# Two decoder layers on one core: where the route weights are made and how alpha x enters the sums

## The chip, the cores and the metric

The kernel runs on one core of a Trainium2 chip, and the metric is the time of one execution on the device in microseconds. PE is TensorE, DVE is VectorE, ACT is ScalarE, POOL is GpSimd and SP is SyncE, which here only issues DMAs. A median of three runs is given, and one profiled execution, from which all rows come.

## What is computed

Two post-norm layers over 256 tokens of width 1024 in fp32. Layer 0 mixes with a gated MLP and latent attention, layer 1 with sparse attention; each mixer is followed by a norm, then a mixture of 32 experts (4 groups of 8; one group, two experts of it for a token) and another norm.

```python
def reference(x, ...):
    for layer in range(DEPTH):
        mix = ab_mixer(x, ...) if layer % 2 == 0 else nsa_mixer(x, ...)
        x = layer_norm(DN_ALPHA * x + mix, ln1_g[layer], ln1_b[layer])
        ffn = hier_moe(x, moe_w_rg[layer], ..., moe_w_down[layer])
        x = layer_norm(DN_ALPHA * x + ffn, ln2_g[layer], ln2_b[layer])
    return x
```

`hier_moe` takes the group by argmax, the two best experts of the group, and weights their outputs with the softmax over the two times the group's probability. Both sums that a norm takes contain alpha x.

## The kernel before

All weights come from HBM through one ring of 23 places of 1 MB in SBUF (class `Ring`). `free` gives places back and `pump` at once issues the next loads in a fixed order on SP, so a load starts when a place is free and SP has come to it. Each layer's experts take 96 such loads: 8 quads of 4 experts, each 8 pieces for the gate and up products and 4 for the down product.

The tokens stand in two halves of 128 (t = 0, 1), and x in two halves of 512 columns (`HALF`). `project` multiplies the mixer's output with its output weights into four PSUM tiles `acc[t][h]`. For each half `products(t, 0)` opens them with `mm(acc[t][h], aident, x[:, t, HALF[h]], True, False)`, where `aident` is the identity times alpha, so alpha x enters by PE; then products with the weights, split into a high and a low part, follow (`mm3`). Most steps of `project` are placed among the mixer's own work by the automatic scheduler; from `close_mixer` on the order is the one written out by hand, and each engine executes its instructions in that order.

`close_mixer` takes the sums out of PSUM (`raw`: ACT copies to x, DVE's statistics read PSUM), normalises without gain and bias, computes the router's logits by PE, and `route` finds the experts on DVE (the maxima, and the one-hot sums in `selb`). `route` returns a function `weights`, which makes the route weights `w32` later. `rank` numbers the tokens of each expert, `places` makes one-hot matrices of a quad's token places (L1358), and `pick` selects the quad's tokens from x with them on PE, in two halves of the depth, each evacuated from PSUM (L1383, L1385 with gain and bias, otherwise L1377). Two functions are left for later: the second half of the first selection together with the four steps `affine`, which put gain and bias on x, and `rest`, which calls both `weights` (L1254 to L1264) and then `back`. It also opens the expert sums `acc2` with matmuls by the zero matrix `zerob`.

`moe_layer` runs the quads. `quad(i)` calls `gate_up`, 8 steps k of gate and up products; before each step `between(k)` runs small work: in quad 0 the functions left over (from k = 4 on), the additions of the quad before into the expert sums (`scatter`, at k = 2 and 4), and the one-hots of the next quad (`places`, at k = 4). After them comes, in quad 0, `rest`; then `activate` on ACT and DVE, the next quad's selection (`pick`, 32 products), the turning of the hidden values (`turn_hidden`, L1449), in quad 0 the products of `aident` with x into the expert sums, `back` for the next quad, and `down`. `back` multiplies the one-hots with the route weights on DVE (L1393), transposes the one-hots on PE (L1397), adds up the weights for each place by four one-column products, and copies the results (L1401, L1403). Most matmuls are issued in the helper `mm`, line 182. Between the sixth and the seventh quad a branch (L1299) looks whether an expert got more tokens than its places hold.

Of the kernel before, what the change touches and what calls it, by code (L numbers as in the profile page):

```python
# [142 lines left out]
def trunk(ctx, tc, a, out):  # L143
# [109 lines left out]
    aident = consts.tile([128, 128], F32, name="aident")  # L253
    idb = consts.tile([128, 128], BF16, name="idb")
    zerob = consts.tile([128, 128], BF16, name="zerob")
# [11 lines left out]
    def more_constants():  # L267
# [4 lines left out]
        V.memset(zerob, 0.0)  # L272
        V.tensor_scalar(aident, ident, ALPHA, None, op0=ALU.mult)
# [174 lines left out]
    def project(l):  # L448
# [7 lines left out]
        def products(t, i):  # L456
            k = ks[i]
            if i == 0:
                for h in range(2):
                    mm(acc[t][h], aident, x[:, t, HALF[h]], True, False)  # L460
            y = [part[:, t * 128:(t + 1) * 128] for part in ys[k]]
            for h in range(2):
                w = held[i][h] if i in SMALL else [part[:, HALF[h]] for part in held[i]]
                mm3(acc[t][h], y, w, False, i == KC - 1)
# [11 lines left out]
    def close_mixer(l, rb, acc, step, products):  # L476
# [4 lines left out]
        def raw(t):  # L481

            for h in range(2):
                S.activation(x[:, t, HALF[h]], acc[t][h], AF.Copy)
            return x[:, t], *stats(acc[t])
# [41 lines left out]
        for h in range(2):  # L527
            mm(acc2[0][h], zerob, idb[:, None, :].to_broadcast([128, 4, 128]), True, False)
        warm(2)
# [5 lines left out]
        for h in range(2):  # L535
            mm(acc2[1][h], zerob, idb[:, None, :].to_broadcast([128, 4, 128]), True, False)
        warm(W1[0])
# [11 lines left out]
        def rest():  # L549
            weights0()  # L550
            weights1()
            return (xg, *back(0, rt, dd, "O"))

        return rt, acc2, (xg, [second] + affines, rest)
# [835 lines left out]
    def back(q, rt, dd, tr, often=True):  # L1390

        d, dw = dd[:, 0:256], (p2() if dd.shape[1] == 256 else dd[:, 256:512])[:, 0:256]
        V.tensor_tensor(dw.rearrange("p (t e s) -> p t e s", t=2, e=4), d.rearrange("p (t e s) -> p t e s", t=2, e=4),  # L1393
                        rt[1][:, :, 4 * q:4 * q + 4, None].to_broadcast([128, 2, 4, 32]), op=ALU.mult)
        p = ps(tr)
# [13 lines left out]
    def gather(q, rt, base, tr):  # L1409
# [5 lines left out]
        return xg, *back(q, rt, dd, tr, often)  # L1415
# [62 lines left out]
    def moe_layer(l, rt, acc, begun):  # L1478
# [3 lines left out]
        gs, late = [(begun[0], None, None)], begun[1:]  # L1482
# [7 lines left out]
        def quad(i):  # L1490
# [4 lines left out]

            def between(k):
                nonlocal rb
                if i == 0 and k >= KC // 2:
                    late[0].pop(0)()
                    if k == KC - 1:  # L1500
                        late[0].pop(0)()
                if k in (2, 4):
                    flush(2)
                if k == 4:
                    dds.append(places(nq, rt, 0.0))
                if k == 5 and i == 3 and l == 0:
# [3 lines left out]
            if i == 0:  # L1510
                gs = [late[1]()]
            hs = activate(hp, [g[2] for g in gs])
            ngs, hts = [], None
            for c in range(nn):
                xg = halves_of(w4())
                pick(dds[c], xg)()
# [176 lines left out]
```

## Time and profile before

| what | us |
|---|---|
| median of 3 runs (700.06 to 701.95) | 700.41 |
| the profiled execution | 700.38 |
| its span, first to last instruction | 698.7 |
| PE busy in it | 619.1 |
| DVE busy | 284.3 |
| ACT busy | 204.5 |

The span holds the first mixer up to about 111 us, its routing up to 120, the experts of layer 0 up to about 323, the second mixer up to 468, its routing up to 477, and the experts of layer 1 up to about 687, with the last norm behind them. PE's busy time counts matmuls whose ends are modelled and overlap. The mean granted clock is 0.956 of 2.4 GHz.

### The profile page before, as it was taken

The page shows a single profiled execution, that of the slowest core. Times are in us where ns is not written, and L with a number is a line of the kernel's source. Part 1 is how long each engine was busy: PE and PEld are TensorE (multiplying, and loading weights), DVE is VectorE, ACT ScalarE, POOL GpSimd, SP SyncE. Part 2 cuts the span into 40 slices and gives each one's busy share as a digit, 9 for nine tenths or more (in the row PEclk, how much of TensorE's full clock was granted, in tenths as well). Part 3 has the DMA queues.
Part 4 walks back from the last instruction along what each step waited for, and adds up shares of the span by engine and source line. Part 5 has one row for each costly group of instructions (what it writes and reads, how often), then busy time and mean ns, then how long its engine had stood idle before and what let it go on. Part 6 is the DMA issues. An engine that isn't in the chain of part 4 may idle for free. (4 is left out here: it accounts for less than half of the span.)

```text
span 698.7 us, 11137 instructions
## 1 busy us (share of the span) xinstructions
PE 619.1 (89%) x4459; PEld 386.7 (55%) x4459; DVE 284.3 (41%) x709; ACT 204.5 (29%) x514; POOL 49.6 (7%) x56
## 2 busy tenths in 40 slices
PE   7799999799999685887999999999799899897883
PEld 5678676464555141423988776685554554644331
DVE  4757736522222120206848897444422212312116
ACT  5554534121111010103546676431111111202011
POOL 4611000000000000002420000000000000000002
PEclk9999999989999988997999999999899999999797
DMA  8946879949999999999498450399689999999961
GB/s 344 418 184 247 334 264 380 398 189 425 419 420 418 423 420 416 421 420 416 161 422 342 127 235 1 129 394 401 280 353 420 420 422 421 420 419 422 414 266 60
DMA packets 34068, 235.62 MB, mean 337 GB/s; under 512 B 3920, under 2 KB 4688, under 8 KB 6224
## 3 DMA queue, kind: packets, MB, share of 16 engines
q1 hardware_dynamic: 34000, 234.75, 82.7%
q8 instruction: 38, 0.62, 0.4%
q14 instruction: 30, 0.25, 0.1%
HBM read 233.69 MB, written 1.05 MB: 336 GB/s over the span
## 5 line engine op out<-in xcount | busy, mean ns | idle before, releaser
L182 PE MATMUL psC<-ring,w 128*32 128x512 f32 (+1 forms) x1040 | 132.5, 618 | 24.5 <-PEq L1299 13.1
L182 PEld LDWEIGHTS psC<-ring,w 128*32 128x32 f32 (+1 forms) x1040 | 31.2, 114 | 90.0 <-issue 48.5
L182 PE MATMUL psA<-ring,ring 128*128 128x256 f32 (+1 forms) x480 | 80.1, 315 | 0.0
L182 PE MATMUL psT<-ring,p 128*32 128x512 f32 (+1 forms) x608 | 68.8, 587 | 3.1 <-DMA ring<-in_moe 2.2
L182 PEld LDWEIGHTS psA<-ring,ring 128*128 128x128 f32 x480 | 67.5, 193 | 6.5 <-issue 1.8
L182 PEld LDWEIGHTS psT<-p,x 128*128 128x128 f32 x512 | 64.5, 208 | 10.9 <-issue 10.1
L182 PE MATMUL psT<-p,x 128*128 128x128 f32 x512 | 67.3, 295 | 0.0
L1437 DVE SCALAR_TENSOR_TENSOR p<-p,psC 128x256 f32<-128x256 f32 x16 | 6.7, 421 | 133.5 <-ACT p L1436 133.3
L317 DVE TENSOR_TENSOR p<-psT,p 128x256 fp32r<-128x256 f32 x72 | 30.5, 424 | 62.8 <-ACT p L316 62.8
L1436 ACT ACTIVATE p<-psC 128x256 f32<-128x256 f32 x16 | 6.1, 383 | 170.2 <-PE psC L182 170.2
L316 ACT ACTIVATE p<-psT 128x256 fp32r<-128x256 f32 x72 | 27.5, 383 | 63.2 <-PE psT L182 42.2
L290 POOL TENSOR_TENSOR sm<-sm,mhalf 128x1 f32<-128x1 f32 (+1 forms) x12 | 7.7, 647 | 511.4 <-DVE sm L287 280.6
L182 PEld LDWEIGHTS psA<-p,k 128*128 128x128 f32 x144 | 25.2, 192 | 30.1 <-issue 17.6
L182 PE MATMUL psA<-p,k 128*128 128x256 f32 x144 | 39.4, 313 | 1.6 <-DVE sm L1560 1.6
L312 DVE TENSOR_TENSOR ring<-ring,ring 128x1024 fp32r<-128x1024 f32 (+1 forms) x28 | 36.0, 1301 | 8.0 <-ACT ring L311 7.7
L182 PEld LDWEIGHTS psT<-ring,p 128*32 128x32 f32 x608 | 17.3, 111 | 37.6 <-issue 25.3
L182 PE MATMUL psS<-ring,ring 128*128 128x416 f32 (+3 forms) x128 | 32.0, 384 | 2.0 <-ACT ring L311 1.5
L182 PE MATMUL psO<-ring,ring 128*64 128x256 f32 (+3 forms) x248 | 32.2, 349 | 1.1 <-DVE ring L333 0.7
L311 ACT ACTIVATE ring<-ring 128x1024 fp32r<-128x1024 f32 (+1 forms) x32 | 31.8, 1031 | 3.6 <-issue 1.3
L182 PE MATMUL psS<-p,k 128*128 128x256 f32 x144 | 29.9, 288 | 0.0
L1377 DVE COPY w<-psT 128x512 f32<-128x512 f32 x16 | 11.1, 691 | 44.2 <-PE psT L182 44.2
L1111 ACT ACTIVATE ring<-psS,sm 128x128 f32<-128x128 f32 (+1 forms) x64 | 26.2, 420 | 7.8 <-DVE sm L1102 7.7
(282 smaller groups left out, 844.4 us busy)
## 6 DMA issues: line engine op xcount, KB each, us to landing
ring<-in_moe SPq DMA_DIRECT2D x192, 1024.0 KB, 19.5
ring<-in_m SPq DMA_DIRECT2D x23, 1024.0 KB, 10.0
ring<-in_vec SPq DMA_DIRECT2D x2, 1024.0 KB, 18.1
ring<-in_m SPq DMA_DIRECT2D x2, 832.0 KB, 6.0
x<-in_x SPq DMA_DIRECT2D x2, 512.0 KB, 5.2
out<-x SPq DMA_DIRECT2D x4, 256.0 KB, 2.0
ring<-in_m SPq DMA_DIRECT2D x1, 768.0 KB, 15.0
ring<-in_m SPq DMA_DIRECT2D x1, 736.0 KB, 18.9
```

The source lines that it names most:

```text
L182: T.matmul(o, lhsT, rhs, start=start, stop=stop, skip_group_check=True)
L290: G.tensor_tensor(r, t, mhalf[:, :n], op=ALU.pow)
L311: S.activation(hi, src, AF.Copy)
L312: (sub or V).tensor_tensor(lo, src, hi.bitcast(F32), op=ALU.subtract)
L316: S.activation(hi, src, AF.Copy)
L317: V.tensor_tensor(lo, src, hi.bitcast(F32), op=ALU.subtract)
L1111: S.activation(p[:, i * w:(i + 1) * w], sx[c, u][:, i * w:(i + 1) * w], AF.Exp, bias=nb[:, i0 + i:i0 + i + 1], accum_out=su[:, i0 + i:i0 + ...
L1377: (S.activation(dst, p[0], AF.Copy) if f == 0 else V.tensor_copy(dst, p[0]))
L1436: S.activation(e, p[:, 0:256], AF.Tanh, scale=0.5)
L1437: V.scalar_tensor_tensor(e, e, 1.0, p[:, 0:256], op0=ALU.add, op1=ALU.mult)
```

## The change

The products with `aident` and with `zerob` go, and with them both constants. In `raw` DVE adds alpha x to the mixer's sum and writes x, and the statistics read x. The expert sums are begun by ACT, which writes alpha x into the PSUM tiles (`residual`: the first half of the columns at k = 7 of the first quad, the second after the next quad's `back`). The route weights and their product with the first quad's one-hots (`shares`) are made at k = 1 of the first quad's products. In all quads the one-hots are multiplied with the weights where they are made (`onehots`, `weighted`), and `back` finds them ready. In place of the `zerob` products as many warming matmuls stand. `router_prep` of the second layer moves from the fourth quad to the sixth. The scratch for dynamic DMAs is 1024 in place of 512.

```diff
         def products(t, i):
             k = ks[i]
-            if i == 0:
-                for h in range(2):
-                    mm(acc[t][h], aident, x[:, t, HALF[h]], True, False)
...
-                mm3(acc[t][h], y, w, False, i == KC - 1)
+                mm3(acc[t][h], y, w, i == 0, i == KC - 1)
...
         def raw(t):
             for h in range(2):
-                S.activation(x[:, t, HALF[h]], acc[t][h], AF.Copy)
-            return x[:, t], *stats(acc[t])
+                V.scalar_tensor_tensor(x[:, t, HALF[h]], x[:, t, HALF[h]], ALPHA, acc[t][h], op0=ALU.mult, op1=ALU.add)
+            return x[:, t], *stats([x[:, t, HALF[h]] for h in range(2)])
...
-        for h in range(2):
-            mm(acc2[0][h], zerob, idb[:, None, :].to_broadcast([128, 4, 128]), True, False)
-        warm(2)
+        warm(4)
...
-        for h in range(2):
-            mm(acc2[1][h], zerob, idb[:, None, :].to_broadcast([128, 4, 128]), True, False)
-        warm(W1[0])
+        warm(W1[0] + 2)
...
-        def rest():
+        def shares():
             weights0()
             weights1()
-            return (xg, *back(0, rt, dd, "O"))
-
-        return rt, acc2, (xg, [second] + affines, rest)
+            return weighted(0, rt, dd, p2()[:, 0:256])
+
+        return rt, acc2, (xg, [second] + affines, shares, lambda dw: (xg, *back(dd, dw, "O")))
...
-    def back(q, rt, dd, tr, often=True):
-
-        d, dw = dd[:, 0:256], (p2() if dd.shape[1] == 256 else dd[:, 256:512])[:, 0:256]
+    def weighted(q, rt, d, dw):
+
         V.tensor_tensor(dw.rearrange("p (t e s) -> p t e s", t=2, e=4), d.rearrange("p (t e s) -> p t e s", t=2, e=4),
                         rt[1][:, :, 4 * q:4 * q + 4, None].to_broadcast([128, 2, 4, 32]), op=ALU.mult)
+        return dw
+
+    def back(d, dw, tr, often=True):
+
         p = ps(tr)
...
+            def residual(h):
+                for t in range(2):
+                    S.activation(acc[t][h], x[:, t, HALF[h]], AF.Copy, scale=ALPHA)
+
+            def onehots(c):
+                dd = places(nq, rt, -32.0 * c)
+                dds.append((dd[:, 0:256], weighted(nq, rt, dd[:, 0:256], dd[:, 256:512])))
+
             def between(k):
                 nonlocal rb
+                if i == 0 and k == 1:
+                    late[1] = late[1]()
                 if i == 0 and k >= KC // 2:
                     late[0].pop(0)()
                     if k == KC - 1:
                         late[0].pop(0)()
+                        residual(0)
                 if k in (2, 4):
                     flush(2)
                 if k == 4:
-                    dds.append(places(nq, rt, 0.0))
-                if k == 5 and i == 3 and l == 0:
+                    onehots(0)
+                if k == 5 and i == 5 and l == 0:
                     rb = router_prep(1, "T")
 
             hp = gate_up(l, q, [g[0] for g in gs], between)
             if i == 0:
-                gs = [late[1]()]
+                gs = [late[2](late[1])]
             hs = activate(hp, [g[2] for g in gs])
             ngs, hts = [], None
             for c in range(nn):
                 xg = halves_of(w4())
-                pick(dds[c], xg)()
+                pick(dds[c][0], xg)()
                 if c + 1 < nn:
-                    dds.append(places(nq, rt, -32.0 * (c + 1)))
+                    onehots(c + 1)
                 if c == 0:
                     hts = turn_hidden(hs)
-                    if i == 0:
-                        for t in range(2):
-                            for h in range(2):
-                                mm(acc[t][h], aident, x[:, t, HALF[h]], False, False)
-                ngs.append((xg, *back(nq, rt, dds[c], "O")))
+                ngs.append((xg, *back(*dds[c], "O")))
+            if i == 0:
+                residual(1)
```

## Rows read from the trace of the kernel before

**Rows 1.** Page, part 2: GB/s of the DMAs in 40 equal slices of the span

```profile
GB/s 344 418 184 247 334 264 380 398 189 425 419 420 418 423 420 416 421 420 416 161 422 342 127 235 1 129 394 401 280 353 420 420 422 421 420 419 422 414 266 60
```

**Rows 2.** Stretches: length, busy us (instructions) by engine, granted clock, DMA share, GB/s

```profile
140.00:150.00 10.00, 10.00 (x43) 8.23 (x43) 2.08 (x5) 1.64 (x4) 0.00 (x0) 0.69 0.41 168
150.00:160.00 10.00, 10.00 (x86) 4.39 (x85) 2.28 (x6) 1.92 (x5) 0.00 (x0) 1.00 0.70 270
...
500.00:510.00 10.00, 10.00 (x66) 5.82 (x69) 1.61 (x4) 2.13 (x5) 0.00 (x0) 0.94 0.16 50
```

**Rows 3.** The same columns for single microseconds of layer 0's hole

```profile
143.00:144.00 1.00, 1.00 (x7) 1.00 (x6) 0.00 (x0) 0.20 (x1) 0.00 (x0) 0.50 0.71 295
...
146.00:147.00 1.00, 1.00 (x9) 0.95 (x8) 0.26 (x1) 0.04 (x1) 0.00 (x0) 0.94 0.02 8
...
152.00:153.00 1.00, 1.00 (x12) 0.26 (x8) 0.00 (x0) 0.16 (x1) 0.00 (x0) 1.00 0.28 49
```

**Rows 4.** Timeline, layer 0: start, length, engine, line, operation, count [idle before, releaser]

```profile
134.51 0.44 PE L1397 MATMUL psO<-ident,k 128*128 128x128 f32 x2
...
139.95 6.76 PE L182 MATMUL psT<-p,x 128*128 128x128 f32 x32
...
150.85 3.64 PE L182 MATMUL psT<-ring,p 128*32 128x512 f32 x32
...
151.97 3.76 SPq L124 DMA_DIRECT2D ring<-in_moe  x5
```

**Rows 5.** Timeline of the same stretch in layer 1

```profile
483.07 0.73 DVE L1383 TENSOR_SCALAR w<-psT,col 128x128 f32<-128x128 f32 x2 [4.82 <-PE psT L182]
...
491.10 0.44 PE L1397 MATMUL psO<-ident,k 128*128 128x128 f32 x2
...
495.76 1.02 PE L182 MATMUL psO<-oneh,p 128*128 128x1 f32 x4 [4.23 <-DVE p L1393]
...
496.64 5.94 PE L182 MATMUL psT<-p,x 128*128 128x128 f32 x32
...
506.73 3.64 PE L182 MATMUL psT<-ring,p 128*32 128x512 f32 x32
```

**Rows 6.** Timeline of layer 1's seventh quad, selection to down product

```profile
658.83 3.84 PE L182 MATMUL psT<-p,x 128*128 128x128 f32 x32
...
663.78 0.61 PE L182 MATMUL psO<-oneh,p 128*128 128x1 f32 x4 [0.68 <-DVE p L1393]
664.32 3.64 PE L182 MATMUL psT<-ring,p 128*32 128x512 f32 x32
```

**Rows 7.** Waits (us, times, longest): whole span, then 235 to 262, then 649 to 690

```profile
PE psO L182 <- DVE p L1393: 18.6, 16, 4.2
...
PE psC L182 <- DMA ring<-in_moe: 5.4, 6, 1.4
...
PEld psC L182 <- DMA ring<-in_moe: 0.6, 2, 0.3
```

**Rows 8.** Stretches, products with aident alone: PE, PEld, DVE busy, clock, DMA share, GB/s

```profile
78.00:92.00 14.00, 4.19 (x8) 1.35 (x8) 0.00 (x0) 1.00 0.68 254
418.00:445.00 27.00, 2.14 (x4) 0.61 (x4) 0.00 (x0) 1.00 0.00 1
```

**Rows 9.** Timeline: an addition from PSUM in mixer 0, and layer 1's second token half

```profile
74.01 0.69 DVE L706 SCALAR_TENSOR_TENSOR p<-psC,ring 128x512 f32<-128x512 f32 x1 [0.20 <-PE psC L182]
...
467.44 1.30 ACT L484 ACTIVATE x<-psS 128x512 f32<-128x512 f32 x2 [1.51 <-PE psS L182]
...
468.07 1.39 DVE L413 BATCH_NORM_STATS2 sm<-psS 128x6 f32<-128x512 f32 x2 [1.14 <-ACT x L484]
...
472.16 0.26 DVE L510 SCALAR_TENSOR_TENSOR sm<-psC,sm,sm 128x40 f32<-128x40 f32 x1
```

**Rows 10.** End of layer 1: a microsecond of the stream, and the last down product

```profile
676.00:677.00 1.00, 1.00 (x16) 0.18 (x8) 0.00 (x0) 0.00 (x0) 0.00 (x0) 1.00 0.16 66
...
684.15 1.07 PE L182 MATMUL psT<-ring,p 128*32 128x256 f32 x16
```

More of the change, by code (lines that the diff above doesn't have):

```diff
@@ L252, in trunk @@
     ident = consts.tile([128, 128], F32, name="ident")
-    aident = consts.tile([128, 128], F32, name="aident")
     idb = consts.tile([128, 128], BF16, name="idb")
-    zerob = consts.tile([128, 128], BF16, name="zerob")
     maskb = consts.tile([128, 128], BF16, name="maskb")
@@ L271, in more_constants @@
         V.memset(oneb, 1.0)
-        V.memset(zerob, 0.0)
-        V.tensor_scalar(aident, ident, ALPHA, None, op0=ALU.mult)
         V.tensor_copy(maskb, tri[:, 128:256])
@@ L1414, in gather @@
         pick(dd, xg)()
-        return xg, *back(q, rt, dd, tr, often)
+        return xg, *back(dd[:, 0:256], weighted(q, rt, dd[:, 0:256], dd[:, 256:512]), tr, often)
     def gate_up(l, q, xgs, between):
@@ L1481, in moe_layer @@
         order = QUADS[l]
-        gs, late = [(begun[0], None, None)], begun[1:]
+        gs, late = [(begun[0], None, None)], list(begun[1:])
         pending = []
@@ L1684 @@
     arrays = {f"in_{k}": np.ascontiguousarray(v) for k, v in pack(inputs).items()}
-    nc = _bacc.Bacc("TRN2", target_bir_lowering=False, num_devices=1, dynamic_dma_scratch_size=512)
+    nc = _bacc.Bacc("TRN2", target_bir_lowering=False, num_devices=1, dynamic_dma_scratch_size=1024)
     args = {k[3:]: nc.dram_tensor(k, v.shape, mybir.dt.from_np(v.dtype), kind="ExternalInput").ap()
```

## The prediction

> **What bounds the kernel now.** I read the DMA row of the page first, then busy time by stretch, then the timeline where the DMA falls silent, then the waits. In the expert layers the weight stream runs at about 420 GB/s [rows 1], but it has one hole in each of them: 168 and 270 GB/s in 140 to 160 us, 50 GB/s in 500 to 510 us [rows 2]. The ring is full there: the eight gate/up products of the first quad free eight places, and then nothing is freed until the first down product. In layer 0 the next loads are issued at 151.97, 1.1 us after that product begins at 150.85 [rows 4]; the stream thins out at 143.7, moves next to nothing in 146:147 and begins again in 152:153 [rows 3].
>
> What keeps the down product back is PE's own chain [rows 4, 5]. The quad's last gate/up product is followed at 491.10 by the transposes of `back`; then PE waits 4.23 us, up to 495.76, for the route weights, a chain of small DVE and ACT steps, comes back at half clock, so that 32 selecting products take 5.94 us (6.76 in layer 0) where they take 3.84 at full clock [rows 6], runs the residual products, and reaches the down product at 506.73: 15.63 us. In layer 0 it is 134.51 to 150.85, 16.34 us.
>
> After the hole the two layers differ. In layer 0 PE catches up with the stream and waits for it (5.4 us in 235 to 262) [rows 7]: its end is the stream's end. In layer 1 PE hardly waits for a load up to the end, 0.6 us of weight loads in 649 to 690 [rows 7], and the stream is ahead: its last bytes pass in 676:677, and 1 MB of them, 2.5 us at 420 GB/s, is the layer norm's gains and biases, so the last expert weights are there by about 674.5, while their product begins at 684.15 [rows 10]. 9.6 us are in hand there. So layer 0 gains what the stream gains, layer 1 what PE gains.
>
> **The change part by part.** *Weights and residual in layer 0.* With the weights ready and the residual on ACT, the way from the last gate/up product to the down product is: `back` (two transposes 0.44, four one-column products 0.54, overlapping: 0.8), then what the same chain takes in quad 6 at full clock from the first selecting product at 658.83 to the down product at 664.32, 5.49, less its 0.68 wait [rows 5, 6]: 5.6 us. PE saves 16.34 - 5.6 = 10.7 us. The loads then come out at about 141.3 instead of 151.97, ahead of 143.7, so the hole closes. It is worth (420 - 168) x 10/420 + (420 - 270) x 10/420 = 9.6 us of stream by bytes [rows 2]. The 16 DMA engines do not stop together, and a load is there only with its slowest: by the silence from about 146.5 to 152.5 [rows 3] it is 6 to 7. I take 8.7, nearer to the bytes, since all engines have to carry them; ends 6.5 and 9.6.
>
> *The same in layer 1.* There PE counts: 15.63 - 5.6 = 10.0 us; ends 9.0 and 10.4. The stream moves by (420 - 50) x 10/420 = 8.8 us as well, so PE may gain up to 9.6 + 8.8 = 18.4 before it has to wait.
>
> *Where the weights go.* The chain lasts about as long as PE's wait for it, 4.2 us. It is put on DVE behind the first selection's evacuation and ahead of the second's at 483.07, before which DVE has nothing for 4.82 us [rows 5]; ACT has nothing there either. Cost nothing, cover 0.6 us; behind it stand the second evacuation, the next quad's one-hots and the norm's gains, and PE's products from k = 4 wait for the first of these. If the chain ran longer, every us beyond 0.6 would cost one.
>
> *One-hots times weights earlier in all quads.* PE waited for this multiplication (L1393) 16 times, 18.6 us [rows 7]; the two long waits are counted above, 14 short ones of about 0.7 are left. The multiplication moves to k = 4 beside gate/up products, or ahead of its use by 32 selecting products. In layer 0 PE's time is hidden by the stream: 0. In layer 1 eight waits fall away, 5.6 us; ends 4 and 6.
>
> *Residual on ACT.* Four writes of 128x512 into PSUM a layer. No row shows ACT writing PSUM; the nearest is its copy from PSUM, 1.30 for two [rows 9]. The first two lie under the gate/up products, the others before the first down evacuation, which can't come before four products of the down step are done. A gain excludes itself, since ACT does nothing there now; at double the price the evacuation would be about 1 us late, and the sums that wait for it stand behind two more gate/up products. 0 taken; end 1 us per layer.
>
> *Mixers: alpha x.* Removed from PE: eight 512-column products, 3.4 us by their spacing of 0.43, a layer. In layer 0 they lie in 78 to 92 us [rows 8], where attention's tail still makes PE wait for ACT and DVE; two pairs stand in such waits, two hold up work that is ready, 1.7 us. In layer 1 half of them stand in 418 to 445 us [rows 8], between products that wait for DVE; the rest is earlier, in the same mixer: 0. Ends 0.9 and 3.4, 0 and 1.7. The Trainium skill ("Trainium Kernel Development and Optimization", Performance Expectations) says that matmul busy time is a bad measure because matmuls are pipelined. By busy time alone both layers would give the whole 3.4, and the sum below would be 29.7; the gaps between dependent rows agree with the page.
>
> Added to DVE: two 128x512 sums in place of ACT's copies, 0.69 each by L706, which also reads PSUM. For the second token half ACT's copies started at 467.44 and the statistics at 468.07; now the sums take 1.38 and the statistics follow at 468.8, 0.7 later, and first routing and the logits' scaling at 472.16 stand behind them on DVE [rows 9]. For the first half DVE waits for PE's logits anyway. +0.7 us a layer; ends 0 and 0.8.
>
> *The rest.* Clearing by matmul becomes as many warming matmuls; two constants fall away; `router_prep` of layer 1 moves from quad 3 to quad 5, where PE waits for the stream, and its load stays in place on SP's queue; the larger DMA scratch serves DMAs that GpSimd issues, and the page lists none. All 0.
>
> **Sum.** Layer 0: 8.7 + 1.7 - 0.7 = 9.7. Layer 1: 10.0 + 5.6 + 0 - 0.7 = 14.9. Together 24.6 us. The profiled execution took 700.38 us (span 698.7 and 1.7 around it), the median is 700.41: 675.8 us.
>
> **The rivals.**
> 1. *Layer 1's stream does not move with PE.* If its hole closes on paper only, PE has 9.6 us in hand and then waits: layer 1 gives 9.6 - 0.7 = 8.9, together 18.6, 681.8 us. For it: the stream is saturated from 510 us on. Against it: the hole is silence, with places full.
> 2. *The mixers give all that PE carried*: 3.4 + 1.7 more than 1.7 in sum, 672.4 us.
> 3. *The weights do not move.* DVE works in order; if something ahead of the chain holds it until the second evacuation, only the residual products (3.4 a layer) and the short waits go: 3.4 + 1.0 + 3.4 + 5.6 - 0.7 = 12.7, 687.7 us.
> 4. *Slower: holes in the mixers' tails.* The products taken out were work that PE could do while it waited. A hole of 4.2 us was followed by the lower clock level (granted 0.69 on the mean of 140 to 150 us, so some six of the ten at 1.2 GHz) [rows 2], which cost 2.1 to 2.9 us on 32 products [rows 4 to 6]; hole and clock make about 6.7. Four of them eat up the 24.6, and 703 us result. In 78 to 92 and 418 to 445 us the granted clock is 1.00, 2.4 GHz [rows 8], and what goes there is 3.4 us in a layer, in four pieces: four long holes are unlikely. The Trainium skill ("TensorE: Matmul & The Clock Gate", HAM oscillation) warns of this: idle gaps return the array to half rate. The trace agrees behind the route weights; no row here shows it in the mixers.
>
> **How the numbers follow.** Forecast 0.72; rival 1 0.10; rival 2 0.08; rival 3 0.06; rival 4 0.02; something between 3 and 4 that ends within 0.3% (what a measurement can tell from no change, 2.1 us) 0.02. The ends of the terms: all good 9.6 + 3.4 + 10.4 + 6 + 1.7 = 31, all bad 6.5 + 0.9 + 9 + 4 - 1.6 - 2 = 17. They will not all fall together; 671 to 682 holds most of the forecast and rivals 1 and 2. Faster 0.96, same 0.02, slower 0.02.
>
> **What would show it.** Right: no DMA silence behind the first quad, from about 110 us up to the end of layer 0's experts at 420 GB/s; granted clock 1.00 there; some 5.6 us from the last gate/up product to the down product; no wait for the weighted one-hots; layer 1 without waits for loads. Wrong: a wait of the second selection's evacuation for the weights; PE waiting for loads late in layer 1; the time from the last mixer product to the first gate/up product longer by more than 0.8; holes in the mixers' tails.

## The result: 671.8 us instead of 700.4

The changed kernel takes 671.79 us (median; single runs 668.4 to 673.8) against 700.41 before. The ratio is 0.958, 95% interval 0.954 to 0.9625. A second series of five runs gave 671.57 and a ratio of 0.959 (0.958 to 0.9605). The forecast was 675.8 with a range of 671.0 to 682.0: the sign, the size and the range hold, but the kernel gained 28.6 us where the sum said 24.6. The profiled execution took 672.46 us (span 670.7), so 27.9 us are to be found between the two profiles.

The page's DMA row of the changed kernel (GB/s in 40 slices) and four stretches (length, busy us and instructions by engine, granted clock, DMA share, GB/s), two in each layer behind the first quad's gate/up products, answer [rows 1] and [rows 2]:

```profile
GB/s 346 417 202 249 353 279 362 393 423 419 419 421 421 422 420 415 421 419 421 103 423 414 174 247 7 1 380 380 415 421 419 421 421 421 421 421 418 418 413 95
```

```profile
130.00:140.00 10.00, 10.00 (x91) 7.23 (x93) 4.58 (x10) 3.70 (x9) 0.00 (x0) 1.00 1.02 425
140.00:150.00 10.00, 10.00 (x92) 4.02 (x84) 2.35 (x6) 1.15 (x3) 0.00 (x0) 1.00 1.01 422
490.00:500.00 10.00, 10.00 (x88) 4.82 (x81) 2.18 (x6) 0.77 (x2) 0.00 (x0) 1.00 1.01 422
500.00:510.00 10.00, 10.00 (x91) 5.78 (x93) 3.46 (x9) 2.91 (x7) 0.00 (x0) 1.00 1.02 423
```

Both holes (slices of 189 and 280 in the row of before) are gone: the stream runs at 422 to 425 GB/s, PE is busy throughout, its granted clock is 1.00. The timelines of the same places answer [rows 4] (layer 0, with the next loads on SP's queue) and [rows 5] (layer 1); columns start, length, engine, line, operation, count:

```profile
132.23 0.44 PE L1389 MATMUL psO<-ident,k 128*128 128x128 f32 x2
132.87 3.82 PE L182 MATMUL psT<-p,x 128*128 128x128 f32 x32
137.40 3.64 PE L182 MATMUL psT<-ring,p 128*32 128x512 f32 x32
...
138.52 3.76 SPq L124 DMA_DIRECT2D ring<-in_moe  x5
```

```profile
480.47 0.44 PE L1389 MATMUL psO<-ident,k 128*128 128x128 f32 x2
481.11 3.82 PE L182 MATMUL psT<-p,x 128*128 128x128 f32 x32
485.63 3.64 PE L182 MATMUL psT<-ring,p 128*32 128x512 f32 x32
```

No wait stands between the last gate/up product and the selection any more, the 32 selecting products take 3.82 us, and the way from `back` to the down product is 5.17 us in layer 0 (16.34 before) and 5.16 in layer 1 (15.63). The loads go out at 138.52, 13.4 us earlier than before.

What goes where is best seen by cutting the span into six pieces. The table gives their lengths in us, from starts in the traces: (1) from the span's start to layer 0's last down product; (2) mixer 1, to the last transposition (`transposed`) for the routing; (3) to the first selecting product; (4) to the first quad's last gate/up product; (5) to the first down product of layer 1; (6) the rest. Below the changed kernel stand experiments, told further down. The time of the execution from which the pieces come stands beside the median of all.

| kernel | 1 | 2 | 3 | 4 | 5 | 6 | profiled, us | median, us |
|---|---|---|---|---|---|---|---|---|
| before | 320.81 | 148.65 | 5.87 | 15.13 | 16.15 | 191.92 | 700.38 | 700.41 |
| changed | 307.65 | 149.02 | 6.43 | 16.72 | 5.69 | 185.11 | 672.46 | 671.79 |
| changed, second series | 306.16 | 149.00 | 6.43 | 16.71 | 5.69 | 185.06 | 670.89 | 671.57 |
| a1, weights late | 315.60 | 149.01 | 6.44 | 16.71 | 13.96 | 184.34 | 687.91 | 687.36 |
| a2, residual on PE | 310.79 | 146.26 | 6.44 | 16.71 | 9.12 | 184.88 | 676.03 | 676.74 |
| a3, mixers on PE | 310.00 | 151.39 | 5.88 | 15.12 | 5.69 | 186.86 | 676.79 | 676.21 |
| a4, one-hots late | 309.74 | 146.26 | 6.44 | 16.70 | 6.63 | 191.65 | 679.26 | 679.00 |
| e1, weights only | 313.43 | 151.00 | 5.88 | 15.12 | 9.12 | 191.59 | 688.01 | 687.56 |
| b1, more warming | 306.67 | 148.99 | 6.44 | 15.12 | 5.69 | 184.33 | 669.08 | 669.08 |

From before to the changed kernel: 13.2 us in piece 1, 10.5 in piece 5, 6.8 in piece 6; pieces 2 to 4 lose 0.4, 0.6 and 1.6. So layer 0 gave 13.2 where the sum had 9.7, and layer 1 with its mixer 14.7 where it had 14.9, though made up differently. Two groups of rows of the changed kernel show what was lost. The first is its routing in layer 1 (the second half's choice of experts, the first selection, the first 32 gate/up products), with the stretch around it:

```profile
462.16 0.18 PE L182 MATMUL psT<-selb,trib 128*128 128x32 bf16 x1 [0.85 <-DVE selb L1237]
...
463.23 3.13 PE L182 MATMUL psT<-k,x 128*128 128x128 f32 x16 [0.87 <-DVE sm L1272]
466.29 4.13 PE L182 MATMUL psC<-ring,w 128*32 128x512 f32 x32
```

```profile
460.00:470.00 10.00, 8.28 (x59) 4.60 (x57) 5.68 (x34) 2.85 (x10) 0.00 (x0) 0.83 0.87 339
```

The same places in the trace of before:

```profile
474.38 0.18 PE L182 MATMUL psT<-selb,trib 128*128 128x32 bf16 x1 [0.29 <-DVE selb L1248]
...
475.45 2.02 PE L182 MATMUL psT<-k,x 128*128 128x128 f32 x16 [0.87 <-DVE sm L1283]
```

The wait for the choice of experts is 0.85 us (0.29 before), the clock falls to 1.2 GHz behind it (0.83 on the mean of ten us), and 16 selecting products take 3.13 us where they took 2.02. The second is the start of mixer 1 (VectorE, GpSimd and PE):

```profile
318.61 8.20 POOL L867 TENSOR_TENSOR ring<-ring,ring 128x608 fp32r<-128x608 f32 x4
...
318.89 2.28 DVE L308 TENSOR_TENSOR ring<-ring,ring 128x1024 fp32r<-128x1024 f32 x1 [1.07 <-DMA ring<-in_m]
...
321.10 1.95 DVE L560 SCALAR_TENSOR_TENSOR x<-x,sm,ring 128x512 f32<-128x512 f32 x1
...
323.19 0.63 PE L325 MATMUL psT<-ident,x 128*128 128x128 f32 x4 [2.42 <-DVE x L560]
```

PE waits 2.42 us there for the layer norm's last step on VectorE (L560), which stands behind a split of weights (L308). In the trace of before PE had no such wait, and the split (L312 there) took 1.22 us:

```profile
330.74 1.22 DVE L312 TENSOR_TENSOR ring<-ring,ring 128x1024 fp32r<-128x1024 f32 x1 [0.54 <-ACT ring L311]
330.83 9.27 POOL L878 TENSOR_TENSOR ring<-ring,ring 128x608 fp32r<-128x608 f32 x4
...
334.01 0.63 PE L329 MATMUL psT<-ident,x 128*128 128x128 f32 x4
```

More on both below.

### The profile page after: what moved, and what is told of

It reads as the page before. It is cut to its first block, busy times and chain, and to the rows that moved or that the text cites. A ratio compares the mean times of both kernels' runs of the same rounds, so it can differ in the third digit from the quotient of the medians.

```text
span 670.7 us, 11059 instructions
## 1 busy us (share of the span) xinstructions
PE 604.0 (90%) x4427; PEld 379.2 (57%) x4427; DVE 290.5 (43%) x715; ACT 204.5 (30%) x514; POOL 48.5 (7%) x56
## 5 line engine op out<-in xcount | busy, mean ns | idle before, releaser
L182 PE MATMUL psC<-ring,w 128*32 128x512 f32 (+1 forms) x1040 | 135.0, 628 | 25.6 <-PEq L1288 13.1
L182 PEld LDWEIGHTS psT<-p,x 128*128 128x128 f32 x512 | 60.3, 197 | 11.9 <-issue 10.9
L182 PE MATMUL psT<-p,x 128*128 128x128 f32 x512 | 63.2, 283 | 0.9 <-ACT k L1393 0.9
L312 ACT ACTIVATE p<-psT 128x256 fp32r<-128x256 f32 x72 | 27.6, 385 | 62.5 <-PE psT L182 41.6
L308 DVE TENSOR_TENSOR ring<-ring,ring 128x1024 fp32r<-128x1024 f32 (+1 forms) x28 | 36.3, 1313 | 8.5 <-ACT ring L307 7.1
L182 PEld LDWEIGHTS psT<-ring,p 128*32 128x32 f32 x608 | 17.3, 110 | 40.2 <-issue 27.9
L307 ACT ACTIVATE ring<-ring 128x1024 fp32r<-128x1024 f32 (+1 forms) x32 | 31.9, 1032 | 4.3 <-DMA ring<-in_m 1.4
```

The source lines that it names most:

```text
L182: T.matmul(o, lhsT, rhs, start=start, stop=stop, skip_group_check=True)
L307: S.activation(hi, src, AF.Copy)
L308: (sub or V).tensor_tensor(lo, src, hi.bitcast(F32), op=ALU.subtract)
L312: S.activation(hi, src, AF.Copy)
```

## The experiments

**The four parts, each undone.** Each of the first four kernels is the changed one with one part as it was. (a2, a3 and f1 also have the smaller DMA scratch again; a5 below, which has it too, shows no difference.)

*a1: the route weights made late again.*

```diff
-                if i == 0 and k == 1:
-                    late[1] = late[1]()
...
-                gs = [late[2](late[1])]
+                gs = [late[2](late[1]())]
```

(During the first quad the next quad's one-hots are then weighted later too, since the weights are not there before.)

> The changed kernel (671.8 us) with the route weights back behind the first quad's gate/up products, residual on ScalarE and mixers as changed. Theory: PE waits some 4.2 us for the weights in both layers and its clock falls after that (2.1 to 2.9 us on 32 selecting products), so the way from the last gate/up product to the down product is about 12 us instead of 5.2. Layer 1 loses 6.8 us. In layer 0 the next loads go out some 6.8 us later, at about 145; the stream ran dry 9.2 us after the last gate/up product, so at about 141.4, and a hole of some 4 us is back. Together +10.5: 682 us. Rival A, the hole came from the residual products and not from the weights: at most +2, 674. Rival B, any delay brings back the whole hole of 9.6 us by bytes: 688.

Measured: 687.36 us (684.84 to 687.91), ratio to before 0.981 (0.979 to 0.9825): +15.6. Rows of layer 0 (the wait, the selection, and ten us of the stream):

```profile
137.56 1.01 PE L182 MATMUL psO<-oneh,p 128*128 128x1 f32 x4 [4.23 <-DVE p L1381]
138.43 6.51 PE L182 MATMUL psT<-p,x 128*128 128x128 f32 x32
```

```profile
140.00:150.00 10.00, 9.32 (x67) 6.72 (x69) 1.97 (x6) 3.14 (x7) 0.00 (x0) 0.80 0.30 101
```

The wait of 4.2 us and the selection at half clock are back as foreseen, but the way to the down product is 8.3 us longer (13.96 for 5.69, piece 5), not 6.8, and in layer 0 nearly all of its delay appears in the end: 101 GB/s in 140 to 150 us is (420 - 101) x 10/420 = 7.6 us of stream lost, and piece 1 is 8.0 longer. The estimate of a hole of 4 us was too small: the loads go out at 147.72, not 145. So it is rival B's price, though not for its reason (7.6 us of the hole come back because the delay is that long, not because any delay brings it all back), and rival A is out.

*a2: the residual back on PE, ahead of the first down product.*

```diff
-            if i == 0:
-                residual(1)
+                    if i == 0:
+                        for t in range(2):
+                            for h in range(2):
+                                mm(acc[t][h], aident, x[:, t, HALF[h]], False, False)
```

> The changed kernel with the residual alpha x of the expert sums back on PE (clearing by matmul, eight 512-column products ahead of the first down product). Theory: way 5.2 + 3.4 = 8.6 us. Layer 1 loses 3.4. In layer 0 the loads go out at about 141.8, just where the stream would run dry (141.4), so 0.5 to 1.5 is lost there. Together +4 to +5: 676 us. Rival, ScalarE's writes into PSUM cost as much as they saved elsewhere (evacuations later): 672.

Measured: 676.74 us (675.59 to 677.35), ratio 0.966 (0.965 to 0.968): +4.9 to +5.2, as the theory said. The way is 9.12 us in both layers, 3.4 more. Two stretches in layer 0:

```profile
140.00:142.00 2.00, 2.00 (x23) 1.09 (x25) 0.16 (x1) 0.38 (x1) 0.00 (x0) 1.00 0.48 197
142.00:144.00 2.00, 2.00 (x24) 0.60 (x20) 0.51 (x2) 0.77 (x2) 0.00 (x0) 1.00 0.64 156
```

The stream loses (420 - 197) x 2/420 + (420 - 156) x 2/420 = 2.3 us although the loads go out only 3.2 us later (141.76). So the changed kernel closes the hole with about 1 us to spare. That the total agrees with the theory is partly luck: layer 0 lost more stream than the 0.5 to 1.5 us expected, and piece 2 is 2.8 us shorter in this trace, for a reason that is told under "The start of mixer 1".

*a3: the mixers' alpha x back on PE, ScalarE's copies in place of VectorE's sums.*

```diff
+            if i == 0:
+                for h in range(2):
+                    mm(acc[t][h], aident, x[:, t, HALF[h]], True, False)
...
-                V.scalar_tensor_tensor(x[:, t, HALF[h]], x[:, t, HALF[h]], ALPHA, acc[t][h], op0=ALU.mult, op1=ALU.add)
-            return x[:, t], *stats([x[:, t, HALF[h]] for h in range(2)])
+                S.activation(x[:, t, HALF[h]], acc[t][h], AF.Copy)
+            return x[:, t], *stats(acc[t])
```

> The changed kernel with the mixers' alpha x back on PE and ScalarE's copies in place of VectorE's sums. By the prediction's terms (1.7 and 0 from PE, 0.7 back from VectorE in each layer): +0.3, 672.1 us. By the starts of the mixer's last sums in the trace of the changed kernel (layer 0 earlier by 2.8, the stream's end by 1 to 2 more than the hole; mixer 1 by some 1.0 more than its start): +2 to +3, 674 to 675. Rival 2 of the prediction, all eight products of a layer lie on the path: 6.8 - 1.4 = +5.4, 677.

Measured: 676.21 us (674.59 to 676.79), ratio 0.965 (0.963 to 0.966): +4.4 to +4.6. The prediction's terms (+0.3) are refuted. Piece 1 is 2.4 longer than in the changed kernel's profile, and piece 2 is 2.4 longer; piece 3 is 0.55 shorter (VectorE's sums are gone from the way to the routing) and piece 4 is 1.6 shorter (no fall of the clock in the routing). In piece 6 this execution is 1.8 longer than the changed kernel's; nothing of the edit lies there, 1.2 of it come at the last down products (granted clock 0.71 in 655 to 660 us), and one profile can't tell whether that repeats.

How the products cost what they do can be followed in mixer 0. First the changed kernel, then a3:

```profile
86.49 0.86 PE L182 MATMUL psO<-ring,ring 128*64 128x256 f32 x6
...
89.91 1.52 PE L182 MATMUL psA<-ring,ring 128*128 128x512 f32 x6
```

```profile
86.48 0.86 PE L182 MATMUL psO<-ring,ring 128*64 128x256 f32 x6
...
91.92 1.52 PE L182 MATMUL psA<-ring,ring 128*128 128x512 f32 x6
```

At 86.5 us both are level in the attention's own products. But from 77.6 us to there the changed kernel has run fifteen of the output projection's 512-column products, and a3 six with `aident` and eight of the others. What a3 has not run by then comes behind, and with its last two `aident` products makes 2.0 us here and 2.5 us a group later.

*a4: the one-hots weighted between selection and transposition again, in all quads but the first.*

```diff
-                dds.append((dd[:, 0:256], weighted(nq, rt, dd[:, 0:256], dd[:, 256:512])))
+                dds.append(dd)
...
-                ngs.append((xg, *back(*dds[c], "O")))
+                ngs.append((xg, *back(dds[c][:, 0:256], weighted(nq, rt, dds[c][:, 0:256], dds[c][:, 256:512]), "O")))
```

> The changed kernel with the multiplication of the one-hots by the weights back between the selecting products and the transposes, for every quad but the first. Theory: PE waits some 0.7 us for each; in layer 0 the stream hides it (0), in layer 1 eight of them cost 4 to 6 us: +5.6, 677.4 us. Rival, layer 1 is bound by its stream now (the last expert weights land about 1 us ahead of their product), so that half of the waits at most count: +1 to +3, 673 to 675.

Measured: 679.00 us (678.47 to 679.67), ratio 0.9695 (0.968 to 0.971): +7.2 to +7.4. The waits of PE in layer 1, 485 to 680 us (us, times, longest):

```profile
PE psO L182 <- DVE p L1381: 6.8, 9, 1.0
```

The changed kernel has no wait of this kind in its list. Pieces 5 and 6 are 0.9 and 6.5 longer: all nine waits count in layer 1 (0.46 to 1.02 us each, and slower column products behind them, 7.5 us), and the rival (the stream ends layer 1 already) is out. Piece 1 is 2.1 longer here, but it is 1.8 longer in d1 below (309.49), whose layer 0 is the changed kernel's: no more than 0.3 us of that can be the one-hots'.

**One part alone.** *e1* is the kernel before with nothing but the weights moved to k = 1 (the first diff the other way round, with the residual, the mixers and the later one-hots as before).

> The kernel before (700.4 us) with one part of the change alone: the route weights made at k = 1 of the first quad. Theory: in each layer the wait of 4.2 us and the slow clock behind it (2.7 us on 32 selecting products) go, 6.9 us of the way to the down product. Layer 1 gains them on PE. In layer 0 the loads go out 6.9 us earlier, at about 145, and since the stream loses every us that they are late beyond 143.7 less what a landing takes, it gains all of it and 2 to 3 us of hole stay. Together -13.8: 686.6 us. Rival A, the parts do not overlap at all, so alone it gives what its removal cost (15.6): 685. Rival B, the hole closes only if the residual goes too: -7 to -8, 693.

Measured: 687.56 us (686.58 to 688.01), ratio 0.982 (0.9805 to 0.983): -12.8, a little less than the theory, and both rivals are off. The way to the down product is 9.12 us instead of 16.15 in layer 1, 7.0 less; piece 1 is 7.4 shorter, with a rest of hole in it:

```profile
140.00:150.00 10.00, 10.00 (x69) 4.20 (x68) 2.88 (x7) 2.30 (x6) 0.00 (x0) 1.00 0.84 325
```

(425 - 325) x 10/425 = 2.4 us. Together 7.4 + 2.4 = 9.8: that is what the hole of layer 0 was worth, the 9.6 by bytes. (Two differences cancel in the 7.4: e1's first quad ends 1.3 us later than before's, 135.28 for 133.98, and its last down products are not slowed by 1.2 GHz as before's are. The stream alone, under "Layer 0's hole" below, gives the same.) What is missing to -13.8 is in piece 2, 2.4 us longer than before, though nothing in mixer 1 was touched. That is the next point.

**The start of mixer 1.** Piece 2 comes in two lengths, whatever the edit: 146.3 or 148.6 to 149.0 with the new mixer, 148.7 or 151.0 to 151.4 with the old one. The rows above show why. VectorE's split (L308) and GpSimd's four subtractions (L867) begin within 0.3 us of each other. In the trace of before, in a2 and in a4 the split begins 0.1 to 0.2 us ahead of GpSimd and takes 1.22 to 1.33; in the changed kernel and its repetition, in a1, a3, a5, b1, e1 and f1 it begins 0.28 to 0.29 behind and takes 2.27 to 2.29. No trace with this order of steps departs from that. In before, a2 and a4 PE had run layer 0's last down products at 1.2 GHz and ended behind the stream; in the others it waited for the last load, and the norm came sooner after it, while the split waits for ScalarE's step (L307, 317.80 to 318.86 in the changed kernel) on a load of its own, which had kept ScalarE waiting for 1.36 us. That this is what turns the order round was not tried by itself. The Trainium skill ("SBUF — State Buffer", Who interferes with whom) says that a VectorE instruction with two SBUF inputs and a GpSimd instruction that reads SBUF exclude each other, and that issue order decides who blocks; the rows agree, both ways round. The loser's delay holds up the norm's step behind it, PE waits 2.4 us, and the granted clock is 0.62 and 0.53 in the four us from 323.5. (In e1 and a5 the wait is 1.25 and 1.14 us; in e1 PE's products ahead of it ran slower, and piece 2 is longer all the same.) Two kernels try to avoid it. *c1* moves both steps of the norm for the second half's first columns (t1, h1) ahead of the transposition of (0, 1), and so ahead of the split; the second of them:

```diff
             V.scalar_tensor_tensor(x[:, t, HALF[h]], x[:, t, HALF[h]], mr[t][1], b[:, HALF[h]], op0=ALU.mult, op1=ALU.add)
+            if (t, h) == (0, 1) and ahead == 1:
+                V.scalar_tensor_tensor(x[:, t1, HALF[h1]], x[:, t1, HALF[h1]], mr[t1][1], b[:, HALF[h1]], op0=ALU.mult, op1=ALU.add)
             after(t, h)
```

> The changed kernel with the layer norm of the second token half's first columns ahead of the first split on VectorE at the start of mixer 1. Theory: where GpSimd's products start before that split, it takes 2.28 instead of 1.27 us, the norm's last step is late, PE waits 2.4 us and goes on at 1.2 GHz, 2.8 us in all; with the norm ahead of it the step takes 0.75, not 1.95, and the wait is gone: 0 where the split came first anyway, -2.8 where it did not, -1 to -2 in the median: 670.3 us. Rival, the loss moves to the steps that now stand behind (the low parts of the transposed x come 1 to 2 us later and PE's next products wait for them): 671.8 or above.

Measured: 673.56 us (672.33 to 675.21), ratio 0.961 (0.960 to 0.962): +2, the rival. The wait of 2.42 us is gone and another stands a little later:

```profile
329.85 2.40 PE L182 MATMUL psO<-ring,ring 128*128 128x304 f32 x8 [3.56 <-DVE ring L329]
```

The low parts of the transposed x (L329) now stand behind several splits. *g1* lets the split win instead, by six small copies on GpSimd ahead of its subtractions (on top of b1, below):

```diff
                 G.tensor_tensor(rest, rest, b[:, HALF[1]], op=ALU.add)
+                if ahead == 1:
+                    t_ = k1()
+                    for j in range(6):
+                        G.tensor_copy(t_[:, 32 * j:32 * j + 32], rest[:, 32 * j:32 * j + 32])
```

> The version with four more warming products in layer 1 (669.1 us), and six small copies (128x32) on GpSimd between the layer norm's sums and GpSimd's four subtractions at the start of mixer 1; they compute nothing that is used. Theory: VectorE's first split there starts 0.28 us behind GpSimd's first subtraction, and takes 2.28 us where it takes 1.22 to 1.33 when it starts 0.1 to 0.2 ahead; some 0.9 us of small copies let it start first, the norm's last step comes 1.4 us sooner, PE's wait of 2.4 us and the slow clock behind it go: -2.8 at most, 666.3 us. Rival, what GpSimd's subtractions lose (they end 1 to 2 us later, and PE needs their results further on in the mixer) takes it back: 669.

Measured: 669.70 us (669.15 to 670.07), ratio 0.956 (0.9545 to 0.957), where b1 has 669.08. The mechanism is there and the gain is not:

```profile
319.19 1.26 DVE L308 TENSOR_TENSOR ring<-ring,ring 128x1024 fp32r<-128x1024 f32 x1 [1.09 <-ACT ring L307]
320.38 0.74 DVE L564 SCALAR_TENSOR_TENSOR x<-x,sm,ring 128x512 f32<-128x512 f32 x1
...
330.28 0.54 PE L182 MATMUL psC<-ring,ring 128*128 128x304 f32 x2 [1.27 <-POOL ring L871]
```

Split and norm take 1.26 and 0.74, and PE does not wait for them; but GpSimd's subtractions begin 2.5 us after the norm's sums instead of at once, and PE waits 1.27 us for them at 330.28. Piece 2 is 148.33, 0.7 shorter than b1's, and the medians show nothing of it.

**The clock in the routing.** *b1* fills PE's wait for the second half's choice of experts, in layer 1 alone:

```diff
-        warm(W1[0] + 2)
+        warm(W1[0] + (2, 6)[l])
```

> The changed kernel with four more warming products in layer 1, while PE waits 0.85 us for the second half's choice of experts, which VectorE's sums made 0.57 later. Theory: this longer wait is what brings the clock to 1.2 GHz on the first selecting products (3.13 us for 16 instead of 2.02, in three of the four traces with these sums a fall, in neither of the two without); filled, the selecting products take 2.0 again and the gate/up products 13.2 instead of 13.65: -1.6, 670.2 us. Rival, the fall has nothing to do with this wait: 671.8.

Measured: 669.08 us (668.95 to 670.07), ratio 0.955 (0.954 to 0.9565), against 671.57 for the changed kernel on the same chip (*after_again*): all five runs lie below its five (670.89 to 672.77). This version beats both kernels. In its trace (routing and the stretch around it):

```profile
462.22 2.02 PE L182 MATMUL psT<-k,x 128*128 128x128 f32 x16 [0.87 <-DVE sm L1272]
464.17 3.64 PE L182 MATMUL psC<-ring,w 128*32 128x512 f32 x32
...
460.00:470.00 10.00, 9.13 (x79) 5.45 (x80) 6.02 (x33) 2.65 (x11) 0.00 (x0) 1.00 1.00 395
```

Clock 1.00, 2.02 and 3.64 us, and piece 4 is 15.12 as before the change: 1.6 us as expected. The rest of the 2.5 is not explained by it; the two profiles differ by 0.7 us in piece 6 as well, at the branch. In layer 1's routing the fall of the clock was seen in the changed kernel, its repetition, a1, a2, a4 and a5, and not in c1, which has the same waits of 0.86 and 0.87; with the wait filled (b1, d1, f1, g1) it was not seen, nor with the shorter wait of the old mixer (before, a3, e1). Layer 0's routing has the same two waits in ten of these traces, and there the clock fell in three: a1, a4 and d1, where the 16 products took 2.71, 3.12 and 3.15 us. (The expectation counted three falls in four traces; in layer 1 it is all four.) In d1:

```profile
114.08 3.15 PE L182 MATMUL psT<-k,x 128*128 128x128 f32 x16 [0.87 <-DVE sm L1279]
```

So the fall came in nine of seventeen routings with the longer wait, and in none of eleven with a shorter or a filled one: the longer wait permits it and does not force it. The Trainium skill ("TensorE: Matmul & The Clock Gate", HAM oscillation) says that idle gaps bring the array to half rate; the rows agree where the clock fell, and the eight routings where it did not show that the waits alone don't decide it.

The base of these kernels on the same chip:

> The changed kernel once more, as the base of the next three. 671.8 us by the first four runs, which spread from 668.4 to 673.8. Theory: the spread comes from three places where PE idles or not and is then at 2.4 or 1.2 GHz: the end of layer 0 (1.3 us), the start of mixer 1 (2.8 us), the branch of layer 1 (some 1.7 us); so single runs of 668 to 674 again. Rival, the spread is of the first chip: all within 2 us.

671.57 us, 670.89 to 672.77: within 2 us, the rival. The two profiles of the changed kernel differ by 1.5 us in piece 1 and by less than 0.1 in every other, so none of the three places tells them apart. A fourth does, in mixer 0 and ahead of all products that the change took out. The stretch from 30 to 40 us, in the first profile and in the second:

```profile
30.00:40.00 10.00, 9.62 (x30) 6.88 (x31) 6.04 (x14) 2.12 (x6) 1.75 (x5) 0.66 0.77 293
```

```profile
30.00:40.00 10.00, 9.44 (x37) 6.76 (x36) 5.59 (x13) 2.44 (x6) 1.46 (x5) 0.83 0.90 351
```

The granted clock is 0.66 and 0.83 (1.00 in a4 and d1), and the first quad's last gate/up product comes at 131.71 and 130.35 us. So piece 1 of a single profile carries more than 1 us that no edit made, and the differences of piece 1 above are no better than that; a3's was followed within its own stretch. Whether the run of 668.4 us, which was not profiled, had the clock of d1 there stays open.

*d1* joins b1 and c1:

> Both edits together. Theory: they lie in different places, 100 us apart, and PE carries both to the end, as layer 1 has hardly a wait for loads: -3, 668.7 us. Rival, the stream ends layer 1 by now (the last expert weights land about 1 us ahead of their product), so no more than -1 to -1.5 can be had: 670.5.

675.67 us (673.58 to 677.0), ratio 0.963 (0.9615 to 0.965): slower than either, so neither expectation. Piece 4 is 15.12, as in b1, and piece 2 is 152.97, as in c1, which is worse by 4 us than the changed kernel's; piece 1 is 309.49. c1's edit costs more than it saves. The routing's clock had not fallen in c1's trace, so b1's edit had nothing to win there; why d1 is 2.1 us slower than c1 is not shown.

**Two small ones.** *a5* undoes the place of the router's preparation (quad 3) and the DMA scratch.

> The changed kernel with its two small edits undone: the preparation of layer 1's router in quad 3 instead of 5, DMA scratch 512. Theory: both cost nothing, 671.6 us. Rival, the place of the preparation counts (its products and its PSUM bank stand in PE's way while the stream is behind in quad 3 but not in 5): +0.5 to +1.5, 672.5.

672.18 us (670.77 to 672.52), ratio 0.960 (0.959 to 0.9615) against 0.959 (0.958 to 0.9605): no difference that can be told. *f1* is b1 with alpha x of the second token half back on PE:

```diff
+            if i == 0 and t:
+                for h in range(2):
+                    mm(acc[t][h], aident, x[:, t, HALF[h]], True, False)
```

> The version with four more warming products in layer 1 (669.1 us), and alpha x of the second token half alone back on PE, with ScalarE's copies for it. Theory: PE carries four of the eight products of a layer, half of the 2.4 us that they cost in either layer, 1.2 each; VectorE's 0.57 us of lateness goes, which layer 1 gets back: +1.2 + 0.6 = 1.8, 670.9 us. Rival, VectorE's sums set the routing so firmly that the two cancel: 669.1 or below.

672.06 us (671.86 to 673.9), ratio 0.961 (0.959 to 0.962): +3.0 to b1, where 1.8 was expected. Piece 1 is 308.59 and piece 2 is 150.26, 1.9 and 1.3 more; piece 3 is 6.29, so only 0.15 of the 0.57 comes back. Even half of these products is on the path.

## Why the prediction was right, and where its sum was off

**The bound and the two regimes** were read rightly. Layer 0 ends with its stream and layer 1 with PE: in a1, a2 and e1 layer 0 loses or gains by the bytes of the hole, and layer 1 (pieces 5 and 6) by the length of the way to the down product, within 0.2 to 0.8 us. The changed kernel has no wait of PE for a load between 485 and 665 us.

**Way to the down product.** Forecast 5.6 us, measured 5.2; layer 1 gained 10.5 (piece 5) for 10.0.

**Layer 0's hole.** 8.7 was taken between 6.5 and 9.6; the upper end, the loss by bytes, is right. From 140 to 300 us, first before, then changed:

```profile
140.00:300.00 160.00, 137.48 (x1053) 69.97 (x1052) 30.98 (x73) 23.23 (x57) 1.45 (x2) 0.94 0.96 395
```

```profile
140.00:300.00 160.00, 136.20 (x1042) 64.99 (x1034) 29.99 (x69) 21.26 (x52) 1.45 (x2) 0.93 1.01 420
```

(420 - 395) x 160/420 = 9.5 us (and 9.8 by e1). The reason given for less, that a load is there only with its slowest engine, had no effect that can be seen. The forecast's slack was too generous: it had the loads out at 141.3 and the stream dry from 143.7. They went out at 138.52, but the stream would have thinned out at about 141 (a2), since the first quad itself came 2.3 us earlier.

**Weights and residual cost nothing.** Right. The weights' chain runs from 119.37 to 123.36 on VectorE, and the second selection's evacuation comes after it with a wait for PE of its own:

```profile
122.94 0.42 DVE L1381 TENSOR_TENSOR p<-k,w 128x256 f32<-128x256 f32 x1
124.20 0.73 DVE L1372 TENSOR_SCALAR w<-psT,col 128x128 f32<-128x128 f32 x2 [0.84 <-PE psT L182]
```

The residual, for which no row of before stood, takes 0.59 to 0.60 us for a 128x512 written to PSUM, and the first evacuation behind it begins 2.0 us after the down product, waiting for PE:

```profile
137.78 0.59 ACT L1490 ACTIVATE psA<-x 128x512 f32<-128x512 f32 x1
138.30 0.59 ACT L1490 ACTIVATE psS<-x 128x512 f32<-128x512 f32 x1
139.39 0.38 ACT L312 ACTIVATE p<-psT 128x256 fp32r<-128x256 f32 x1 [0.49 <-PE psT L182]
```

**One-hots.** 5.6 was forecast for layer 1, from eight waits of 0.7. The eight are 0.46 to 1.02 long and 6.1 in all; a4 has a ninth, of 0.68 in the first quad, where before the residual products covered the step. The column products behind a wait are slower (0.61 for 0.50): 7.5 in a4, of which 0.9 lies in piece 5 and was counted there; 6.5 to 6.8 in piece 6 stand against the 5.6. 0 in layer 0: right within 0.3.

**The mixers: the term that failed.** Forecast 1.7 and 0 us of PE's 3.4, because the products stood beside waits. a3 gives 2.4 in piece 1 net of VectorE's part, and 2.4 in mixer 1. In mixer 1 the products were read as lying "between products that wait for DVE"; but without them PE runs other products in their place, as the rows of a3 show for mixer 0, and the last of these sets when VectorE gets the last sum. For mixer 1 that is concluded from a3's 2.4 us and f1's 1.3, not followed product by product. A wait next to a product does not make the product free; only a wait that would have been as much longer without it does. VectorE's part was sized well where it was named (0.56 us, piece 3, for 0.7: two sums of 0.69 in place of ScalarE's copies, the rows answering [rows 9] below), but it had a follower that was not: the clock's fall, 1.6 us in piece 4 of layer 1 (and in some executions of layer 0).

```profile
454.65 1.39 DVE L477 SCALAR_TENSOR_TENSOR x<-x,psS 128x512 f32<-128x512 f32 x2 [0.51 <-PE psS L182]
...
459.93 0.26 DVE L503 SCALAR_TENSOR_TENSOR sm<-psC,sm,sm 128x40 f32<-128x40 f32 x1
```

From the sums to the logits' scaling it is 5.28 us, where it was 4.72 from ScalarE's copies.

**The sum again, with measured terms.** Layer 0: 9.6 of hole, 2.4 of mixer, and 1.2 that were not foreseen: in the trace of before PE runs the last down products of layer 0 at 1.2 GHz and ends behind the stream, in the changed kernel it waits for the last load. First before, then changed:

```profile
316.36 1.94 PE L182 MATMUL psT<-ring,p 128*32 128x256 f32 x16 [0.56 <-DMA ring<-in_moe]
320.24 1.07 PE L182 MATMUL psT<-ring,p 128*32 128x256 f32 x16
```

```profile
307.08 1.07 PE L182 MATMUL psT<-ring,p 128*32 128x256 f32 x16 [0.35 <-DMA ring<-in_moe]
```

Layer 1: 10.5 of way, 6.8 of one-hots, 2.4 of mixer, less 0.6 for VectorE, 1.6 for the clock and 2.8 for the split. 13.2 + 14.7 = 27.9. The 1.2 us are not shown to be the change's: in d1, with the changed layer 0, the last down products ran at 1.2 GHz as well (granted 0.56 in 304 to 310 us), as in a2 and a4. Two losses that were not in the sum (4.4 us) hide how much too low the gains were put. That the time fell into the range is in part their doing: without them it would have been near 667.4 us, below 671.0, and b1, which takes away the clock's 1.6, ran 669.08.

**The rivals.** Rival 1 (layer 1's stream does not move with PE) is refuted: the last down product starts at 656.25, 27.9 us earlier, without a wait for a load; but the stream's last bytes now pass in 656:657, and the last expert weights, issued at 638.99, land 16.2 us later at 655.2, so of the 9.6 us in hand about 1 is left. Rival 2 (the mixers give all that PE carried) named 672.4 us, and the measured 671.8 lies by that number: its mechanism, given 0.08, is the one that holds in the main: in a3 the products cost 4.8 us in pieces 1 and 2 where it had 5.1. The low chance came from reading waits beside the products instead of following the products' own successors. Rival 3 (the weights don't move) is refuted by e1 and a1: they are worth 12.8 alone and 15.6 at last. Rival 4 (holes in the mixers' tails) did not come about where it was put, but a small one of its kind did, 1.6 us, one place later in the routing.

## What to carry to other kernels

A product taken off an engine that sometimes waits is worth nothing only if the wait behind it would grow by as much; undo the one edit and look, before calling it hidden. When work moves to another engine, cost the first wait behind it and the clock after that wait, and fill it with a few warming products: four of them were worth 2.5 us here, 1.6 of it in the place that they filled. Where the first steps after a boundary on VectorE and GpSimd share SBUF, see which starts first. Before two profiles are compared piece by piece, look for places that no edit touches and see by how much those differ.

## What was unexpected of the hardware

- The order of two starts 0.3 us apart decides 1 us on VectorE (1.22 to 1.33, or 2.27 to 2.29 us for the same 128x1024 subtraction) and 2.4 to 2.8 us in the end.
- Behind two waits of 0.85 and 0.87 us on PE with small products between them the granted clock fell in nine of seventeen routings (six of seven in layer 1, three of ten in layer 0): 0.83 on the mean of ten us, 3.13 us for 16 products instead of 2.02 in the changed kernel.
- The same instructions of mixer 0, which no edit touched, ran at a granted clock of 0.66, 0.83 or 1.00 in 30 to 40 us, and the mixer's last transposition began at 110.16, 108.79 and 107.64 us (changed kernel, its repetition, d1).
- ScalarE's write of a 128x512 from SBUF into PSUM takes 0.59 to 0.60 us beside a busy PE.
